# Odd layer of a two-layer encoder: S5 permutes through DRAM, S5 work cut into pieces, mask rows inside the score product

## The chip, the cores and the metric

The kernel runs on one core of one Trainium2 chip. It has five engines, each with its own instruction queue that is worked off in order: TensorE (PE, matrix products into PSUM, with its weight loads shown as PEld), VectorE (DVE), ScalarE (ACT), GpSimd (POOL) and SyncE (SP), which here does nothing but issue DMAs. ACT can issue DMAs too. The metric is the device time of one execution in microseconds (us), the median of several runs. Before the change it is 1480.8 us (three runs, 1479.17 to 1481.18).

## The reference, cut to what matters

Two residual layers over x of shape (512 positions, 1024 features). The even layer is Mamba-2 with differential attention, and a SwiGLU block follows each layer; none of that is edited. The odd layer projects once and feeds two groups:

```
u, c_q, c_kv, k_rope = split_cols(h @ w_in, (512, 384, 256, 32))
# S5: 32 groups of 16 channels, one 64-dim complex state per group
bu    = einsum('bsgh,gph->bsgp', ug, b_bar)
state = associative_scan(h_t = a_bar * h_{t-1} + bu_t)
y     = gelu(real(state @ c^T) + d_skip * ug);  y = y * sigmoid(y @ w_glu + b_glu)
# MLA: 8 heads, 64 plain + 32 rotary dims, block-causal mask in chunks of 64
q  = rms_norm(c_q) @ w_uq;  k_nope, v = split(rms_norm(c_kv) @ w_ukv)
p  = softmax(where(key_chunk <= query_chunk, (q . k) * scale, -inf));  o = p @ v
h  = h + concat(y, o) @ w_out
```

## The kernel before, in words

Activations are held feature-major: tiles of 128 features by 512 positions. Every projection is done in split precision (mm3, L173): weight and input are each cut into a high and a low part, and three products are summed per block of 128 input features, so a unit with 8 blocks is 24 matmuls (L178 to L180). The weights come as one DMA per chunk of one to four units (wload, L153) into one of two `raw` buffers; ACT makes the high part `whi` (L169), DVE the low part `wlo` (L170), each into one of two buffers, so the parts of a unit wait for the unit before last to be multiplied. `drive` (L244) walks a list of units and callbacks, and splits the weights of the next unit just before it writes the products of the present one. The list and a build-time scheduler fix the order of each engine's queue; at run time nothing is reordered.

The odd layer's list (L1475) is: four S5 input units `u`; `ck` twice, `cq` three times (the last of these and the key rotary part `cr` share a chunk); the row statistics of ck and cq (L309 sums of squares by a product with ones, a chain of some ten small DVE instructions, L326 a broadcast back); `values`; then the query and key units of the eight heads in four pairs; the GLU units; the attention steps, woven with the rest; the output units.

S5 is done in four quarters Q. `ev_u` (L1240) multiplies the projection by the row scale into `us`, and then sorts 16 blocks of 32 partitions by 128 columns into `u4` with 16 copies, half on ACT, half on DVE (L1247). `s5a` (L1252) makes eight products into two PSUM banks of the `sc` pair (L1258), four DVE products (L1266 to L1269), two POOL sums (L281), eight DVE scans (L1274), and the rotation back on DVE and POOL (L1284 to L1289). Two units later `s5b` (L1293) makes twelve products, adds the skip (L1305), applies GELU, and sorts blocks back into `yf`, again with 16 copies (L1311).

In an attention step (`scores`, L1392) each of two heads makes one score product with 96 rows (64 plain, 32 rotary; L1397), and a second product of one row that adds -1e30 to the last 64 columns of the first 64 queries (L1399); then a maximum on DVE, the exponential on ACT, and the division by the sum, on DVE for head 0 and on POOL for head 1 (L1405). `flip` transposes, `attend` multiplies by the values.

Of the kernel before, what the change touches and what calls it, by code (L numbers as in the profile page):

```python
# [121 lines left out]
class Trunk:  # L122
# [81 lines left out]

    def compute(self, u):
# [38 lines left out]
    def drive(self, items):  # L244
        us = [x for x in items if isinstance(x, dict)]
        nxt = {id(u): v for u, v in zip(us, us[1:])}
        self.prep(us[0])
        for x in items:
            if isinstance(x, dict):
                if id(x) in nxt:  # L250
                    self.prep(nxt[id(x)])
                self.compute(x)
            else:
                x()
        self.flush()
# [13 lines left out]
    def stat_add(self, st, src, pool=None, tag="sacc"):  # L269
        nc = self.nc  # L270
        if st["acc"] is None:
            st["acc"] = self.t(pool or self.stp, [P, T], tag)
            nc.scalar.activation(out=st["acc"], in_=src, func=AF.Square)
        else:
            sq = self.t(self.tmp, [P, T], "sq")
            nc.scalar.activation(out=sq, in_=src, func=AF.Square)
            self.padd(st["acc"], st["acc"], sq)

    def padd(self, out, x, y, op=ALU.add):
# [90 lines left out]
    def setup(self):  # L370
# [11 lines left out]
        self.n_unit = 0  # L382
        self.raws, self.kept = {}, {}
        self.queue, self.held = [], None
# [832 lines left out]
    def odd(self, E):  # L1217
# [7 lines left out]
        def start():  # L1225
            nonlocal sp
            sp = self.pool(ctx, "od")
            self.norm_done(E)

# [3 lines left out]
        def t5(tag, dt=F32):  # L1233

            return self.t(E["s5p"], [P, T], tag, dt)
# [4 lines left out]
        def ev_u(Q, ps):  # L1240
            us = t2("us", bufs=2)
            V.tensor_tensor(out=us.rearrange("p (i c) -> p i c", i=4), in0=ps.rearrange("p (c i) -> p i c", i=4),
                            in1=E["rbc"].rearrange("p (c i) -> p i c", i=4), op=ALU.mult)
            u4[Q] = t2(f"u4{Q}", shape=[P, 4, P])
            for q in range(4):
                for i in range(4):
                    (A.copy if i % 2 else V.tensor_copy)(out=u4[Q][32 * i:32 * i + 32, q, :],  # L1247
                                                         in_=us[32 * q:32 * q + 32, i * P:(i + 1) * P])

        def v4(x):  # L1250
            return x.rearrange("p (q c) -> p q c", q=4)[:, :, 0:P - 1]

        def s5a(Q):
            S = self.s5
            pb = [self.ps("sc") for _ in range(2)]
            for ri in range(2):
# [13 lines left out]
            self.padd(t[0], t[0], t[1])  # L1270
            self.padd(t[2], t[2], t[3], ALU.subtract)
            for q in range(4):
                for x in (t[0], t[2]):
                    V.tensor_tensor_scan(x[:, q * P:(q + 1) * P],  # L1274
                                         S["r4"][:, 4 * Q + q:4 * Q + q + 1].broadcast_to([P, P]),
                                         x[:, q * P:(q + 1) * P], 0.0, op0=ALU.mult, op1=ALU.add)
            c_, s_ = (S[n][Q].rearrange("p q c -> p (q c)") for n in ("rc", "rs"))
            if Q % 2:
                hr, hi = (t5(f"b{ri}{Q // 2}").rearrange("p (q c) -> p q c", q=4) for ri in range(2))
            else:  # L1280
                hr, hi = t2("hr", shape=[P, 4, P]), t2("hi", shape=[P, 4, P])
# [7 lines left out]
            G.tensor_tensor(out=hi[:, :, 1:P], in0=hi[:, :, 1:P], in1=v4(t[3]), op=ALU.add)  # L1289
            self.later(2, lambda: s5b(Q, hr, hi))  # L1290

        def s5b(Q, hr, hi):
            S = self.s5  # L1293
            ps = self.ps("sc")
# [13 lines left out]
            yf[Q] = t2(f"yf{Q}")  # L1308
            for j in range(4):
                for q in range(4):  # L1310
                    (A.copy if q % 2 else V.tensor_copy)(out=yf[Q][32 * q:32 * q + 32, j * P:(j + 1) * P],  # L1311
                                                         in_=yy[32 * j:32 * j + 32, q * P:(q + 1) * P])

# [61 lines left out]
        def ev_qk(m, n):  # L1375
            def f_(ps):
                if n == 0:
                    qk[m] = [None, None]
                x = qk[m][n] = [t5(f"{('b1', 'rc')[n]}{2 * (m % 2) + hh}") for hh in range(2)]
                for hh in range(2):  # L1380
# [10 lines left out]
        def scores(m, qb):  # L1391
# [15 lines left out]

# [67 lines left out]
        items = [start] + uu  # L1475
# [64 lines left out]
def pack(i):  # L1540
# [27 lines left out]
    def putc(n, v):  # L1568
# [11 lines left out]
    putc("sg64", np.where(r % 64 < 32, -tp, tp)[:, None])  # L1580
    putc("sg32", np.where(r % 32 < 16, -tp, tp)[:, None])
    putc("sel", (r[:, None] % 32 == np.arange(16)[None, :]) & (r[:, None] < 64))
# [3 lines left out]
    arrays = {"xt": i["x"][0].T, "positions": i["positions"], "par": par, "cst": cst, "mask": mask, "cidx": cidx,  # L1586
              "rowp": rowp, "s5bc": bc}
    mats = {n: i[n][0] for n in ("ev_w_in", "ev_w_out", "od_w_in", "od_w_glu", "od_w_uq", "od_w_ukv", "od_w_out")}
# [32 lines left out]
```

## Time and profile before

| | us |
|---|---|
| median of three runs | 1480.8 |
| profiled execution, its own time | 1481.41 |
| its span in the trace | 1479.6 |
| PE busy in the span | 1426.2 (96%) |
| DVE busy | 954.1 (64%) |
| ACT busy | 661.5 (45%) |
| POOL busy | 256.9 (17%) |

The page cuts the span into 40 slices of 37 us. A digit is the busy share of a slice in tenths, and PEclk the clock that TensorE was granted, in tenths of full speed. Only in the slices from about 880 to 990 us, the S5 and latent part of the odd layer, do both fall below 9 in the middle of the span. A matmul's busy time in the trace is longer than its share of the engine, since matmuls overlap; from one start to the next is the better measure.

### The profile page before, as it was taken

What the parts mean: (1) busy time and instruction counts of PE and PEld (TensorE: products, weight loads), DVE (VectorE), ACT (ScalarE), POOL (GpSimd) and SP (SyncE); (2) the same over time, 40 slices, a digit from 0 to 9 for tenths busy, and PEclk for the clock granted to TensorE, in tenths of its full rate; (3) what the DMA queues carried; (4) which work ended last, traced back from release to release, by engine and by line L of the source; (5) the groups of instructions that cost most, each with busy time, mean ns of one, the idle gap of its engine ahead of it and who ended that gap; (6) DMA issues with size and microseconds to landing.
All of it is one profiled execution on the core that took longest, in us unless ns stands there. A gap on an engine that the chain in (4) does not pass through costs nothing.

```text
span 1479.6 us, 18488 instructions
## 1 busy us (share of the span) xinstructions
PE 1426.2 (96%) x7043; PEld 1155.1 (78%) x7043; DVE 954.1 (64%) x1992; ACT 661.5 (45%) x1198; POOL 256.9 (17%) x206
## 2 busy tenths in 40 slices
PE   7999999999999999999999997789999999999997
PEld 5877877788878877888888886666688888888887
DVE  6987788777664999774634469886664433443453
ACT  5658766767544334334223453256453322222342
POOL 0234511000002210011011213523221100100111
PEclk9999999999999999999999998889999999999999
DMA  5221121112212222223222221020122232323221
GB/s 179 78 73 58 61 82 44 59 57 72 86 58 85 102 86 86 86 86 107 96 103 87 98 86 38 24 75 2 62 109 85 89 112 86 108 77 114 86 100 57
DMA packets 20248, 119.80 MB, mean 81 GB/s; under 512 B 2368, under 2 KB 3008, under 8 KB 9024
## 3 DMA queue, kind: packets, MB, share of 16 engines
q1 hardware_dynamic: 18864, 116.86, 22.9%
q10 hardware_dynamic: 1296, 1.76, 0.4%
q8 instruction: 55, 0.90, 0.3%
q14 instruction: 33, 0.27, 0.1%
HBM read 116.52 MB, written 2.10 MB: 80 GB/s over the span
## 4 chain that ended last, share of the span: by engine, by line
PE 74%; DVE 18%; ACT 3%; POOL 2%; issue 2%; DMA 1%; SPq 0%; ACTq 0%; DVEq 0%; POOLq 0%
PE mm L178 14%; PE mm L180 14%; PE mm L179 13%; PE sc L180 7%; PE sc L179 7%; PE sc L178 7%; DVE wlo L170 3%; PE sc L1397 1%; PE sc L813 1%; POOL xs L281 1%; PE po L842 1%; DVE qsw L608 1%; PE mm L750 1%; PE po L1425 1%; PE sc L812 1%
## 5 line engine op out<-in xcount | busy, mean ns | idle before, releaser
L169 ACT CAST whi<-raw 128x1024 fp32r<-128x1024 f32 (+5 forms) x231 | 223.9, 970 | 568.6 <-PE mm L179 331.3
L170 DVE TENSOR_TENSOR wlo<-raw,whi 128x1024 fp32r<-128x1024 f32 (+5 forms) x231 | 266.8, 1155 | 44.2 <-ACT whi L169 31.6
L281 POOL TENSOR_TENSOR gt<-gt,rbc 128x512 f32<-128x512 f32 x44 | 76.3, 1734 | 572.6 <-ACT gt L952 572.6
L957 DVE TENSOR_TENSOR gt<-mm,gt 128x512 f32<-128x512 f32 x44 | 30.3, 690 | 111.3 <-PE mm L180 107.9
L281 POOL TENSOR_TENSOR sacc<-sacc,sq 128x512 f32<-128x512 f32 x29 | 45.4, 1566 | 300.5 <-issue 232.7
L951 DVE TENSOR_TENSOR gt<-sc,rbc 128x512 f32<-128x512 f32 x44 | 30.3, 689 | 88.9 <-PE sc L180 88.9
L180 PE MATMUL mm<-x0h,wlo 128*128 128x512 f32 (+2 forms) x91 | 37.2, 409 | 12.4 <-DVE wlo L170 12.4
L178 PE MATMUL mm<-x0h,whi 128*128 128x512 f32 (+2 forms) x91 | 39.9, 438 | 6.1 <-ACT x0h L343 5.4
L972 DVE TENSOR_TENSOR h<-h,mm 128x512 f32<-128x512 f32 x20 | 13.7, 687 | 44.0 <-PE mm L180 44.0
L768 ACT ACTIVATE qsw<-mm 32x512 f32<-32x512 f32 x64 | 37.7, 589 | 3.1 <-DVE qraw L764 2.3
L972 DVE TENSOR_TENSOR h<-h,sc 128x512 f32<-128x512 f32 x20 | 13.7, 686 | 38.9 <-PE sc L180 38.8
L178 PE MATMUL mm<-x1h,whi 128*128 128x512 f32 (+2 forms) x91 | 36.7, 403 | 1.8 <-ACT x1h L343 1.8
L952 ACT ACTIVATE gt<-gt 128x512 f32<-128x512 f32 x44 | 27.6, 628 | 22.9 <-DVE gt L951 22.9
L180 PE MATMUL mm<-x1h,wlo 128*128 128x512 f32 (+2 forms) x91 | 37.3, 410 | 0.0
L180 PE MATMUL mm<-x2h,wlo 128*128 128x512 f32 (+2 forms) x91 | 37.2, 408 | 0.0
L178 PE MATMUL mm<-x7h,whi 128*128 128x512 f32 (+2 forms) x95 | 37.1, 391 | 0.0
L180 PE MATMUL mm<-x7h,wlo 128*128 128x512 f32 (+2 forms) x95 | 37.1, 391 | 0.0
L179 PE MATMUL mm<-x7l,whi 128*128 128x512 f32 (+2 forms) x95 | 37.0, 390 | 0.0
L179 PE MATMUL mm<-x0l,whi 128*128 128x512 f32 (+2 forms) x91 | 36.8, 405 | 0.2 <-DVE x0l L344 0.2
L179 PE MATMUL mm<-x2l,whi 128*128 128x512 f32 (+2 forms) x91 | 37.0, 407 | 0.0
L179 PE MATMUL mm<-x1l,whi 128*128 128x512 f32 (+2 forms) x91 | 36.8, 404 | 0.2 <-DVE x1l L344 0.2
L178 PE MATMUL mm<-x3h,whi 128*128 128x512 f32 (+2 forms) x91 | 36.8, 405 | 0.0
(938 smaller groups left out, 4385.5 us busy)
## 6 DMA issues: line engine op xcount, KB each, us to landing
raw<-in_f_dram SPq DMA_DIRECT2D x52, 1024.0 KB, 4.8
raw<-in_w_dram SPq DMA_DIRECT2D x35, 1024.0 KB, 4.8
raw<-in_f_dram SPq DMA_DIRECT2D x16, 896.0 KB, 4.5
raw<-in_w_dram SPq DMA_DIRECT2D x8, 512.0 KB, 3.6
h<-in_xt_dram SPq DMA_DIRECT2D x8, 256.0 KB, 6.8
raw<-in_w_dram SPq DMA_DIRECT2D x2, 640.0 KB, 3.9
out_dram<-otm SPq DMA_DIRECT2D x4, 256.0 KB, 2.5
out_dram<-otm ACTq DMA_DIRECT2D x4, 256.0 KB, 2.9
```

Source lines behind the costliest of these rows:

```text
L169: nc.scalar.copy(out=hi[:, :n], in_=raw[:, o:o + n])
L170: nc.vector.tensor_tensor(out=lo[:, :n], in0=raw[:, o:o + n], in1=hi[:, :n].bitcast(F32), op=ALU.subtract)
L178: nc.tensor.matmul(ps, lhsT=hi[:, k, :m], rhs=xh, start=start and j == 0, stop=False)
L179: nc.tensor.matmul(ps, lhsT=hi[:, k, :m], rhs=xl, start=False, stop=False)
L180: nc.tensor.matmul(ps, lhsT=lo[:, k, :m], rhs=xh, start=False, stop=stop and j == n - 1)
L281: self.nc.gpsimd.tensor_tensor(out=out, in0=x, in1=y, op=op)
L608: V.scalar_tensor_tensor(out=acc, in0=xr[:, 1 + k:1 + k + T], scalar=self.par("cw", 12 * k + j), in1=acc, op0=ALU.mult, op1=ALU.add)
L768: A.activation(out=sw[c * 32:(c + 1) * 32, :], in_=ps[d * 32:(d + 1) * 32, :], func=AF.Identity, scale=scale)
L951: V.tensor_tensor(out=gt, in0=ps, in1=E["rbc"], op=ALU.mult)
L952: A.activation(out=gt, in_=gt, func=AF.Silu)
L957: V.tensor_tensor(out=gt, in0=ps, in1=gt, op=ALU.mult)
L972: V.tensor_tensor(out=self.h[i], in0=self.h[i], in1=ps, op=ALU.add)
```

## The change

- `regroup` (new): the 16 copies of a block sort become one DMA of the tile (128 by 512, 256 KB) to a DRAM scratch tile and four DMAs back, each 32 partitions by 4 by 128 elements (64 KB). All five are issued by SP. It serves `u4` and `yf` of all four quarters: eight times, 40 DMAs.
- `s5a` becomes a generator in four pieces (products; scans; rotation back; second products with GELU), and the list places each piece. Its first products go to the PSUM pair `po`. Quarters 1 and 3 use other buffers for their result.
- `drive` counts the units left of each weight chunk and calls `fetch` before each unit, so that a chunk's DMA is written as soon as one of the two `raw` buffers has no unit left.
- The mask becomes four more rows of the score product (96 to 100), loaded by eight DMAs of 8 KB on ACT's queue into the query and key tiles of pairs 0 and 1; pairs 2 and 3 use the same tiles again. The one-row product goes.
- The division of head 1 goes from POOL to ACT.

The order of the engines' queues differs from before only between the odd layer's first units and its last attention steps (and in one mask load at the start).

```
+    def fetch(self):
+        for k in self.order:
+            if k not in self.raws:
+                if sum(self.left[x] > 0 for x in self.raws) >= 2:
+                    return
+                self.raws[k] = self.wload(k)
...
+    def regroup(self, out, src):
+        d = self.t(self.dram, [P, T], "regroup", bufs=4)
+        self.nc.sync.dma_start(out=d, in_=src)
+        for i in range(4):
+            self.nc.sync.dma_start(out=out[32 * i:32 * i + 32],
+                                   in_=d.rearrange("(q p) (i c) -> p i q c", q=4, i=4)[:, i])
...
             u4[Q] = t2(f"u4{Q}", shape=[P, 4, P])
-            for q in range(4):
-                for i in range(4):
-                    (A.copy if i % 2 else V.tensor_copy)(out=u4[Q][32 * i:32 * i + 32, q, :],
-                                                         in_=us[32 * q:32 * q + 32, i * P:(i + 1) * P])
+            self.regroup(u4[Q], us)
...
-            pb = [self.ps("sc") for _ in range(2)]
+            pb = [self.ps("po") for _ in range(2)]
...
             self.padd(t[2], t[2], t[3], ALU.subtract)
+            yield
             for q in range(4):
                 for x in (t[0], t[2]):
                     V.tensor_tensor_scan(x[:, q * P:(q + 1) * P],
...
-            self.later(2, lambda: s5b(Q, hr, hi))
-
-        def s5b(Q, hr, hi):
-            S = self.s5
+            yield
             ps = self.ps("sc")
...
+            self.regroup(yf[Q].rearrange("p (j c) -> p j c", j=4), yy)
...
+                if m < 2:
+                    x = [t5(f"{('b1', 'rc')[n]}{2 * (m % 2) + hh}") for hh in range(2)]
+                    for hh in range(2):
+                        A.dma_start(out=x[hh][96:100, :], in_=a["cmask"][4 * n:4 * n + 4, :])
+                else:
+                    x = qk[m - 2][n]
...
-                PE.matmul(ps[:, :n], lhsT=qk[m][0][hh][0:96, qb * P:(qb + 1) * P], rhs=qk[m][1][hh][0:96, :n],
-                          start=True, stop=False)
-                PE.matmul(ps[:, n - 64:n], lhsT=self.mrow, rhs=self.nrow, start=False, stop=True)
+                PE.matmul(ps[:, :n], lhsT=qk[m][0][hh][0:100, qb * P:(qb + 1) * P],
+                          rhs=qk[m][1][hh][0:100, :n], start=True, stop=True)
...
-            for hh, e in enumerate((V, G)):
-                e.tensor_scalar(out=pp[hh][:, :n], in0=pp[hh][:, :n], scalar1=rr[:, hh:hh + 1], scalar2=None,
-                                op0=ALU.mult)
+            V.tensor_scalar(out=pp[0][:, :n], in0=pp[0][:, :n], scalar1=rr[:, 0:1], scalar2=None, op0=ALU.mult)
+            A.mul(out=pp[1][:, :n], in_=pp[1][:, :n], mul=rr[:, 1:2])
...
-        items += [L(s5a, 0), uck[0], L(s5a, 1), uck[1], lambda: self.later(1, rows_k, rows_k2), ucq[0], L(s5a, 2),
-                  ucq[1], ucq[2], L(s5a, 3), lambda: self.later(1, rows_q, rows_q2)] + ukr
-        items += [uv, uqr(0)] + uqk(0) + uqk(1) + [uqr(1)]
+        items = [start] + uu[:3] + [s5(0), uu[3], s5(0), uck[0], s5(1, 0), uck[1], lambda: self.later(1, rows_k, rows_k2),
+                                    s5(1), ucq[0], s5(1), s5(0), ucq[1], s5(2), ucq[2], s5(2, 1),
+                                    lambda: self.later(1, rows_q, rows_q2)]
+        items += ukr + [s5(3, 2), uv, s5(3, 2), uqr(0), s5(3)] + uqk(0) + [s5(3)] + uqk(1) + [uqr(1)]
```

Three places in the queues. First SP, at the start of the odd layer; before, it holds weight chunks alone (`raw`):

```order
L157 DMA raw_7733<-in_w_dram 128x2048
L157 DMA raw_7857<-in_w_dram 128x2048
L157 DMA raw_8018<-in_w_dram 128x2048
L157 DMA raw_8226<-in_w_dram 128x1280
L157 DMA raw_8381<-in_w_dram 128x1408
```

Now, from the chunk of the first two cq units on, the block sorts of the four `u` quarters stand among the chunks, and then that of the first `yf`:

```order
L157 DMA raw_7797<-in_w_dram 128x2048
L298 DMA regroup_7778<-us_7775 128x512
L298 DMA regroup_7787<-us_7784 128x512
L300 DMA u_1443_7777<-regroup_7778 32x4x128 x4
L300 DMA u_1446_7786<-regroup_7787 32x4x128 x4
L298 DMA regroup_7827<-us_7824 128x512
L298 DMA regroup_7885<-us_7882 128x512
L157 DMA raw_7903<-in_w_dram 128x1280
L300 DMA u_1453_7826<-regroup_7827 32x4x128 x4
L300 DMA u_1465_7884<-regroup_7885 32x4x128 x4
L157 DMA raw_8014<-in_w_dram 128x1408
L298 DMA regroup_8102<-us_8095 128x512
```

SP works in order, so a `raw` that stands behind a sort waits for what the sort waits for, and a sort's reads wait for its write to land.

Second DVE, from the last `u` unit to the low part of the first ck unit (`us`: scaled projection; `t`: S5's working tiles; `rc`, `rs`: its rotation tables):

```order
L1247 COPY u_1455_7890<-us_7888 32x128 x8
L1266 TENSOR_TENSOR t_1458_7917<-sc_7907,rc_1132_5514 128x512
L1267 TENSOR_TENSOR t_1459_7918<-sc_7908,rs_1133_5515 128x512
L1268 TENSOR_TENSOR t_1460_7919<-sc_7908,rc_1132_5514 128x512
L1269 TENSOR_TENSOR t_1461_7920<-sc_7907,rs_1133_5515 128x512
L1274 SCALAR_TENSOR_TENSOR t_1458_7917<-s5r_1063_5005,t_1458_7917 128x128 x4
L1274 SCALAR_TENSOR_TENSOR t_1460_7919<-s5r_1063_5005,t_1460_7919 128x128 x4
L1284 TENSOR_TENSOR hr_7935<-t_1458_7917,rc_1132_5514 128x4x127
L1286 TENSOR_TENSOR hi_7936<-t_1460_7919,rc_1132_5514 128x4x127
L1288 TENSOR_TENSOR hr_7935<-hr_7935,t_1459_7918 128x4x127
L170 TENSOR_TENSOR wlo_7946<-raw_7857,whi_7945 128x1024
L344 SCALAR_TENSOR_TENSOR ck0l_7975<-mm_7949,par_94,ck0h_7974 128x512
```

Now (`po` in the place of `sc`):

```order
L1267 TENSOR_TENSOR us_7882<-mm_7857,rbc_7768 128x512
L170 TENSOR_TENSOR wlo_7900<-raw_7690,whi_7899 128x1024
L1289 TENSOR_TENSOR t_1457_7843<-po_7833,rc_1133_5516 128x512
L1292 TENSOR_TENSOR t_1460_7846<-po_7833,rs_1134_5517 128x512
L1290 TENSOR_TENSOR t_1458_7844<-po_7834,rs_1134_5517 128x512
L1291 TENSOR_TENSOR t_1459_7845<-po_7834,rc_1133_5516 128x512
L1298 SCALAR_TENSOR_TENSOR t_1457_7843<-s5r_1064_5007,t_1457_7843 128x128 x4
L1298 SCALAR_TENSOR_TENSOR t_1459_7845<-s5r_1064_5007,t_1459_7845 128x128 x4
L1310 TENSOR_TENSOR hr_7956<-t_1457_7843,rc_1133_5516 128x4x127
L1312 TENSOR_TENSOR hi_7957<-t_1459_7845,rc_1133_5516 128x4x127
L1314 TENSOR_TENSOR hr_7956<-hr_7956,t_1458_7844 128x4x127
L170 TENSOR_TENSOR wlo_7967<-raw_7797,whi_7966 128x1024
```

The copies are gone, the `wlo` of the second ck unit has moved ahead of quarter 0's products, and the `wlo` behind quarter 0 is that of the first cq unit.

Third PE, around the sum of squares of ck (`tp<-ones,sacc`); before, it stands behind the second products of quarter 1 (`sc<-u,tt`, `sc<-b,cx`) and ahead of those of quarter 2's first ones:

```order
L1298 MATMUL sc_8127<-b_1476_8008,cx_1144_5592 128x128
L1300 MATMUL sc_8127<-b_1477_8009,cx_1145_5593 128x128
L309 MATMUL tp_8163<-ones_97,sacc_7978 128x1 x4
L1258 MATMUL sc_8188<-u_1449_7840,b_1191_6065 128x128 x4
L178 MATMUL mm_8232<-x0h_7425,whi_8092 128x512
```

Now, behind the last products of the first cq unit and ahead of quarter 0's second products:

```order
L179 MATMUL mm_8016<-x7l_7673,whi_7966 128x512
L180 MATMUL mm_8016<-x7h_7672,wlo_7967 128x512
L333 MATMUL tp_8047<-ones_97,sacc_7934 128x1 x4
L1320 MATMUL sc_8082<-u_1443_7777,tt_1122_5429 128x128
L1321 MATMUL sc_8082<-hr_7956,cx_1095_5190 128x128
L1323 MATMUL sc_8082<-hi_7957,cx_1096_5191 128x128
```

The statistic has moved ahead of quarter 0's and quarter 1's second products and ahead of the second cq unit.

## Rows read from the trace of the kernel before

**Rows 1.** Windows: length, PE, PEld, DVE, ACT, POOL busy (count), PEclk, DMA share, GB/s.
```profile
882.00:988.00 106.00, 83.84 (x412) 67.66 (x411) 89.49 (x184) 41.33 (x88) 40.70 (x33) 0.87 0.11 36
988.00:1012.00 24.00, 23.22 (x111) 16.01 (x109) 20.04 (x33) 17.75 (x31) 6.83 (x5) 1.00 0.14 53
1012.00:1080.00 68.00, 68.00 (x399) 45.66 (x399) 41.44 (x94) 32.92 (x87) 16.22 (x14) 1.00 0.13 47
```
**Rows 2.** PE's waits from 882 to 1012 us: total, times, longest.
```profile
PE mm L180 <- DVE wlo L170: 12.1, 4, 6.1
PE tp L326 <- DVE rkr L319: 4.8, 1, 4.8
PE mm L178 <- DVE b L1382: 3.5, 1, 3.5
```
**Rows 3.** Timeline of PE: start, length, instruction.
```profile
882.02 1.95 PE L1258 MATMUL sc<-u,b 128*128 128x128 f32 x16
883.72 0.48 PE L178 MATMUL mm<-x0h,whi 128*128 128x512 f32 x1
...
889.26 1.95 PE L1258 MATMUL sc<-u,b 128*128 128x128 f32 x16
```
**Rows 4.** The chain that ended last: start, length, what; a matmul after a wait.
```profile
913.08 0.43 PE mm L178
```
**Rows 5.** Timeline of DVE, quarters 0 and 1 of S5.
```profile
885.25 0.69 DVE L1266 TENSOR_TENSOR t<-sc,rc 128x512 f32<-128x512 f32 x1
...
887.95 4.76 DVE L1274 TENSOR_TENSOR_SCAN t<-s5r,t 128x128 f32<-128x128 f32 x8 [0.21 <-POOL t L281]
...
895.47 2.27 DVE L170 TENSOR_TENSOR wlo<-raw,whi 128x1024 fp32r<-128x1024 f32 x1
897.66 0.74 DVE L344 SCALAR_TENSOR_TENSOR ck0l<-mm,par,ck0h 128x512 fp32r<-128x512 f32 x1
...
910.74 0.74 DVE L344 SCALAR_TENSOR_TENSOR ck1l<-mm,par,ck1h 128x512 fp32r<-128x512 f32 x1
```
**Rows 6.** Timeline of ACT.
```profile
911.51 0.60 ACT L276 ACTIVATE sq<-mm 128x512 f32<-128x512 f32 x1 [4.98 <-DVE ck1l L344]
912.12 1.28 ACT L1307 ACT_TABLE_LOAD   x1
913.42 0.63 ACT L1307 ACTIVATE us<-us 128x512 f32<-128x512 f32 x1
```
**Rows 7.** Timeline of POOL.
```profile
912.18 1.27 POOL L281 TENSOR_TENSOR sacc<-sacc,sq 128x512 f32<-128x512 f32 x1 [2.37 <-ACT sq L276]
...
960.05 2.51 POOL L1330 TENSOR_TENSOR cx<-us,rope_cos 32x512 f32<-32x512 f32 x1
962.64 3.02 POOL L1332 TENSOR_TENSOR cx<-cx,hi 32x512 f32<-32x512 f32 x1
```
**Rows 8.** Windows of lines L1247 and L1311, the copies: length, DVE, ACT busy.
```profile
870.00:988.00 118.00, 6.96 (x32) 9.50 (x32) 0.88 0.12 41
882.00:988.00 106.00, 7.94 (x32) 9.48 (x32) 0.87 0.11 36
```
**Rows 9.** DMA issues: count, KB each, median us from issue to landing.
```profile
raw<-in_w_dram SPq DMA_DIRECT2D x35, 1024.0 KB, 4.8
...
out_dram<-otm SPq DMA_DIRECT2D x4, 256.0 KB, 2.5
...
cidx<-in_cidx_dram SPq DMA_DIRECT2D x1, 64.0 KB, 3.0
```
**Rows 10.** Timeline of SP at the start: four issues in a row.
```profile
1.16 1.84 SPq L409 DMA_DIRECT2D h<-in_xt_dram  x4
```
**Rows 11.** Line L1399, the mask product: count, ns; and two rows of PE's timeline.
```profile
L1399 PE MATMUL sc<-nrow,mrow x32: 197/198/199, 999.0 to 1071.4; 1*128 1x64 bf16 x32
...
1017.00 0.20 PE L1399 MATMUL sc<-nrow,mrow 1*128 1x64 bf16 x1
1017.13 0.44 PE L1415 MATMUL tp<-cst,rs 128*128 128x128 f32 x2
```

More of the change, by code (lines that the diff above doesn't have):

```diff
@@ L200, in prep @@
         o = sum(CH[u["key"]][2][:u["sub"]])
+        self.left[u["key"]] -= 1
         u["w"] = self.wsplit(self.raws[u["key"]], o, u["nk"], u["m"], u["keep"])
@@ L246, in drive @@
         nxt = {id(u): v for u, v in zip(us, us[1:])}
+        seen = set()
+        for u in us:
+            if u["keep"] is None or u["keep"] not in seen:
+                self.left[u["key"]] = self.left.get(u["key"], 0) + 1
+            seen.add(u["keep"])
+        self.order = list(self.left)
         self.prep(us[0])
@@ L251, in drive @@
                     self.prep(nxt[id(x)])
+                self.fetch()
                 self.compute(x)
@@ L382, in setup @@
         self.n_unit = 0
-        self.raws, self.kept = {}, {}
+        self.raws, self.kept, self.left = {}, {}, {}
         self.queue, self.held = [], None
@@ L1227, in start @@
             sp = self.pool(ctx, "od")
+            self.dram = self.pool(ctx, "swap", space=bass.MemoryType.DRAM)
             self.norm_done(E)
@@ L1276, in s5a @@
                                          x[:, q * P:(q + 1) * P], 0.0, op0=ALU.mult, op1=ALU.add)
-            c_, s_ = (S[n][Q].rearrange("p q c -> p (q c)") for n in ("rc", "rs"))
-            if Q % 2:
-                hr, hi = (t5(f"b{ri}{Q // 2}").rearrange("p (q c) -> p q c", q=4) for ri in range(2))
+            yield
+            if Q == 1:
+                hr, hi = (t5(f"b{ri}0").rearrange("p (q c) -> p q c", q=4) for ri in range(2))
+            elif Q == 3:
+                hr, hi = (t2(f"t{ri}", shape=[P, 4, P]) for ri in range(2))
             else:
@@ L1289, in s5a @@
             G.tensor_tensor(out=hi[:, :, 1:P], in0=hi[:, :, 1:P], in1=v4(t[3]), op=ALU.add)
-            self.later(2, lambda: s5b(Q, hr, hi))
-        def s5b(Q, hr, hi):
-            S = self.s5
+            yield
             ps = self.ps("sc")
@@ L1308, in s5b @@
             yf[Q] = t2(f"yf{Q}")
[L1309 to L1312, printed above, removed]
+            self.regroup(yf[Q].rearrange("p (j c) -> p j c", j=4), yy)
         cq, ck = [None] * 3, [None] * 2
@@ L1378, in f_ @@
                     qk[m] = [None, None]
-                x = qk[m][n] = [t5(f"{('b1', 'rc')[n]}{2 * (m % 2) + hh}") for hh in range(2)]
+                if m < 2:
[4 more added lines that the diff above has]
+                    x = qk[m - 2][n]
+                qk[m][n] = x
                 for hh in range(2):
@@ L1474, in odd, with s5, f_ @@
         uv = self.unit("vq", 0, None, None, body=values)
-        items = [start] + uu
-        items += [L(s5a, 0), uck[0], L(s5a, 1), uck[1], lambda: self.later(1, rows_k, rows_k2), ucq[0], L(s5a, 2),
-                  ucq[1], ucq[2], L(s5a, 3), lambda: self.later(1, rows_q, rows_q2)] + ukr
-        items += [uv, uqr(0)] + uqk(0) + uqk(1) + [uqr(1)]
+        gens = {}
+        def s5(*Qs):
+            def f_():
+                for Q in Qs:
+                    if Q not in gens:
+                        gens[Q] = s5a(Q)
+                    next(gens[Q], None)
+            return f_
+        items = [start] + uu[:3] + [s5(0), uu[3], s5(0), uck[0], s5(1, 0), uck[1], lambda: self.later(1, rows_k, rows_k2),
+                                    s5(1), ucq[0], s5(1), s5(0), ucq[1], s5(2), ucq[2], s5(2, 1),
+                                    lambda: self.later(1, rows_q, rows_q2)]
+        items += ukr + [s5(3, 2), uv, s5(3, 2), uqr(0), s5(3)] + uqk(0) + [s5(3)] + uqk(1) + [uqr(1)]
         steps = [(m, qb) for m in range(4) for qb in (3, 2, 1, 0)]
@@ L1581, in pack @@
     putc("sg32", np.where(r % 32 < 16, -tp, tp)[:, None])
+    cm = np.zeros((8, T), f)
+    for b in range(4):
+        cm[b, P * b:P * b + 64] = 1.0
+        cm[4 + b, P * b + 64:P * b + P] = NEG
     putc("sel", (r[:, None] % 32 == np.arange(16)[None, :]) & (r[:, None] < 64))
@@ L1586, in pack @@
     arrays = {"xt": i["x"][0].T, "positions": i["positions"], "par": par, "cst": cst, "mask": mask, "cidx": cidx,
-              "rowp": rowp, "s5bc": bc}
+              "rowp": rowp, "s5bc": bc, "cmask": cm}
     mats = {n: i[n][0] for n in ("ev_w_in", "ev_w_out", "od_w_in", "od_w_glu", "od_w_uq", "od_w_ukv", "od_w_out")}
```

## The prediction

> **What bounds the kernel now.** I read the page's slices first: PE is busy 9 tenths or more nearly everywhere, and in the stretch that the change reorders (the S5 and latent part of the odd layer) it is not. The windows put numbers to it [rows 1]: from 882 to 988 us PE is busy 83.84 of 106 us, so 22.2 us are idle, and the granted clock is 0.87; from 988 (the GLU units) to 1080 PE is busy without a gap worth the name, at clock 1.00. The waits say what PE lacked [rows 2]: four times the low part of a weight, 12.1 us, the longest 6.1; once `rkr`, the end of the ck statistic, 4.8; once an attention operand, 3.5. That is 20.4 of the 22.2 us.
>
> A matmul after a wait starts every 0.43 us [rows 4]; between waits a unit of 24 takes 889.26 - 883.72 = 5.54 us, 0.23 each [rows 3]. These fit the two clock levels, 1.2 and 2.4 GHz. A mean of 0.87 between 0.5 and 1.0 means up to 13.8 us lost to the low level (0.13 x 106); some of it falls in idle time, so I take 12.5, or 2.1 for each of the six waits. What remains of the stretch is PE's work at full clock: 106 - 22.2 - 12.5 = 71.3 us.
>
> Why `wlo` is late shows in DVE's timeline [rows 5]. From 885.25 DVE works off a quarter of S5 (products, scans 4.76, rotation); the `wlo` that PE wants stands behind it at 895.47. A quarter's chain up to `ck0l` lasts 897.66 + 0.74 - 885.25 = 13.15 us, two of them up to `ck1l` 26.2 us. DVE is 84% busy (89.49 of 106), so the stretch is a contest between DVE's chain and the order in which PE asks for things.
>
> **The change, part by part.** The profiled execution took 1481.41 us (median 1480.8); the sum is made against it.
>
> *Sorts.* The copies go: in 882 to 988 us 7.94 us of DVE and 9.48 of ACT for `yf`, 6.96 and 9.50 for `u4` [rows 8]. The `u4` copies lay beside the products of the `u` units, so PE gains nothing from them directly. In their place stand five DMAs per sort. No such round trip is in the trace; by the nearest rows a 256 KB store lands in 2.5 us, a 64 KB load in 3.0 [rows 9], and SP needs 0.46 per issue [rows 10]: 2.5 + 4 x 0.46 + 3.0 = 7.3 us. From below: 64 KB pieces of data that is already at hand could take no longer than the store, so 5; from above, where it stands behind a 1 MB chunk (4.8, rows 9) 7.3 + 4.8 = 12.1. I take 7.3, nearest to rows of the same size, plus the chunk for the first sort. The first `u4` sort has its chunk ahead of it and the reads land at about 883 to 884, when PE has the last `u` unit behind it and wants them: hidden to within a microsecond. The others have a unit or more (5.54 each) as cover; without it each would cost its 7.3.
>
> *Pieces.* I laid PE's new order from 882.0, with the same 71.3 us of work. DVE's chain starts about 885.0, since `wlo` of the second ck unit (2.27, rows 5) now stands ahead of it; so the 6.1 us wait disappears, and other things are late next:
> 1. The first cq unit wants a bank that `ck0l` and ACT's square empty: 885.0 + 13.15 + 0.6 (the products are taken in another order) + 0.60 [rows 6] = 899.4. PE gets there at 882.0 + 2 x 5.54 + two of `s5a`'s product sets at 1.7 (883.72 - 882.02, rows 3) = 896.5. Hole 2.9.
> 2. The ck statistic now stands right behind that unit and ahead of quarter 0's second products, so a wait is added with the rest of PE's queue behind it. It needs `ck1l` (885.0 + 26.2 = 911.2), the square 0.60 and POOL's sum 1.27 [rows 7]: 913.1. PE is there at 899.4 + 5.54 + 2.1 (low level after the hole) = 907, or 905 if less of it is low. Hole 6 to 8, taken as 6.8, with hole 1's loss of clock hidden in it.
> 3. The cq statistic, behind the last cq and the key unit: 0.7.
> 4. `yf` of an early quarter comes by DMA, and ACT's cast of it stands ahead of the emptying of a bank: 1.2.
> 5. The cq row waits for `rqr`, which stands on DVE behind quarter 3's scans, and these behind POOL's rotation of the key, 2.51 + 3.02 [rows 7]; the mask DMAs on ACT's queue wait at the same time for tiles that S5 frees. Hole 3.1; its bounds are 0 (POOL early) and 5.5 (all of POOL's two steps).
> Holes 2.9 + 6.8 + 0.7 + 1.2 + 3.1 = 14.7; low level after holes 2 and 5, 2 x 2.1 = 4.2. The GLU units start at 882.0 + 71.3 + 14.7 + 4.2 = 972.2 instead of 988: gain 15.8.
>
> *GLU and first attention.* From 988 to 1012 us ACT was busy 17.75 of 24, PE 23.22 [rows 1]. ACT now also has six of the 16 divisions of head 1 (at most 0.60 each, the square of the same tile size, rows 6: 3.6) and, since exponential, sigmoid and GELU alternate there, three more table loads of 1.28 [rows 6], 3.8. 17.75 + 7.4 = 25.2 is more than the stretch: ACT becomes the bound in it. Loss between 0 (the casts are elsewhere by then) and 4.5 (every load in front of PE); I take 2.5. In the trace the next activation follows 0.02 us after the load's end [rows 6]. The Trainium skill speaks against this part: "ScalarE: Activation LUTs", section "What ACT_TABLE_LOAD costs", gives about 2.66 us for each switch, load and drain together. By it the three switches would cost about 4 us more (3 x 1.38), and the estimate would be 1469; this trace shows no such drain, so the sum stays with 1.28.
>
> *Mask.* 32 one-row products go. Each shows 198 ns, but from its start to the next product's it is 0.13 us [rows 11]. Six of them fall before 1012, the other 26 into a stretch in which PE is all that counts (68.00 of 68, rows 1): 26 x 0.13 = 3.4 us. The longer contraction (100 rows for 96) streams as many columns, and I cost it at nothing. The eight 8 KB DMAs take ACT 8 x 0.46 = 3.7 us at SP's rate, beside PE's work (counted in 5 where they are not). The divisions after 1012 find ACT at 32.92 of 68.
>
> *Early weight DMAs* cost nothing while two chunks are in hand; no wait of [rows 2] is for a chunk, so nothing is gained.
>
> Sum: -15.8 + 2.5 - 3.4 = -16.7, 1464.7 against the profiled execution, 1464 to 1465 by the median. I say 1465; this likeliest case by itself spans 1456 to 1473: downwards hole 2 at 2 and hole 5 at nothing (4.8 + 3.1), upwards both at their upper ends (1.2 + 2.4), the GLU loss at 4.5 (2.0) and one sort uncovered by its chunk (4.8 at most, of which I count half).
>
> **The rivals.** *DVE's chain decides.* It begins no earlier (885.0 for 885.25), and if DVE has little slack through four quarters, PE only waits elsewhere; what is left is the mask, 4 us, and a little more: 1475 to 1478. For it: DVE is busy 89.49 of 106, and hole 2 is the old chain under another name. Against it: 7.94 us of copies leave DVE in just this stretch.
>
> *ACT or the round trip holds.* ACT's queue stops at a cast of `yf` that has not landed or at a mask DMA, twice for 3 to 4 us, with 2.1 of low clock after each: 10 us of the gain go, 1475. For it: SP's order puts chunks behind sorts, ACT now mixes DMAs with casts. Against it: ACT is idle for 61% of the stretch.
>
> *Nearly everything is won.* All idle time, all low clock and the masks would give 1481.4 - 22.2 - 12.5 - 4.1 = 1442.6; if hole 2 shrinks to 2 and 5 vanishes, 1455 or lower, about 1452. For it: removed DVE work is 15 us with the `u4` copies. Against it: `ck1l` at about 911 rests on DVE's durations.
>
> *Slower: the sorts come in series on PE's path.* Eight sorts at 7.3 us, each with 2.1 of low clock where it stops PE. The sum gives 16.7 us away to spend: from the second sort that is not hidden at all (2 x 9.4 = 18.8) the change loses. Two: 1483.5; three: 1493. For it: SP works in order, reads wait for the write's landing, a late sort delays the chunk behind it and with it the next unit. Against it: a sort's consumer is a unit or more away, and two chunks are in hand.
>
> *The change does not do what it says:* the one-row products gone but the holes unmoved is the first rival; I give it no chance of its own.
>
> **How the numbers follow.** Likeliest case 0.58; DVE's chain 0.12; ACT or round trip 0.13; nearly everything 0.09; slower 0.08. What a measurement of this kernel can tell from no change is about 0.2%, 3 us. Faster by more than that: all cases but the slower one, 0.92, less 0.05 of the DVE case that ends at 1478 or just above and so within the 0.2%, and less 0.01 of the ACT case, should its stops be twice as long; 0.86. No change 0.05, slower 0.08 + 0.01 = 0.09. The range leaves out the slower case and the far end of the good one: 1452 to 1478.
>
> **What would show it.** Right: no wait ahead of the second ck unit; a wait of about 3 us ahead of the first cq unit, for DVE's `ck0l` or ACT's square; one of 6 to 8 us at the ck statistic, ended by POOL's sum; about 3 at the cq row; sorts of 2.5 and 3.0 us; GLU at about 972; six table loads; attention as full of PE as before. Wrong: waits that end with a sort's DMA, or with a weight chunk (rival four); ACT stopped at a mask DMA for more than 4 us with PE behind it; a GLU start before 965 or after 980; or a ck statistic that finds `ck1l` done, which would mean that DVE's chain starts or runs earlier than I read.

## The result and the profile after

The changed kernel takes 1461.45 us (four runs, 1458.52 to 1462.28) against 1480.03 before: ratio 0.987, 95% interval 0.9853 to 0.9888, so 18.6 us less. The prediction was 1465, with a range of 1452 to 1478. The profiled execution spans 1460.5 us, 19.1 less than that of before.

The windows of the trace after, cut at the events of [rows 1] (the first is the S5 part and ends where the GLU units start, the second ends where the score products of the second pair of heads begin, the third where the last attention product starts):

```profile
880.60:972.40 91.80, 79.18 (x412) 65.96 (x411) 75.99 (x141) 28.46 (x46) 39.73 (x33) 0.91 0.23 75
972.40:1002.00 29.60, 25.38 (x118) 18.38 (x116) 20.68 (x40) 24.47 (x43) 2.95 (x2) 0.88 0.17 58
1002.00:1060.80 58.80, 58.80 (x357) 43.49 (x355) 39.85 (x90) 37.18 (x96) 0.00 (x0) 1.00 0.15 55
```

Before, cut at the same events (the first of the three windows is in [rows 1]):

```profile
988.00:1014.70 26.70, 25.92 (x132) 17.93 (x130) 21.90 (x37) 19.97 (x38) 7.52 (x5) 1.00 0.13 47
1014.70:1079.60 64.90, 64.90 (x375) 43.54 (x373) 39.33 (x89) 30.30 (x81) 15.53 (x13) 1.00 0.14 50
```

The cuts stand at the same events, but the work between them is not quite the same: the last six products of a key unit (two blocks of L178 to L180, 0.23 us each, 1.4 in all) lie ahead of the second cut before, and behind it now. Their first one, before and after:

```profile
1002.44 0.39 PE L178 MATMUL mm<-ck0h,whi 128*128 128x512 f32 x1
1004.75 0.50 PE L178 MATMUL mm<-ck0h,whi 128*128 128x512 f32 x1
```

The reader is to see three things. The S5 part is 14.2 us shorter (106.0 to 91.8), with the same 412 matmuls, less DVE (89.49 to 75.99) and less ACT. The GLU part is 2.9 longer, 4.3 for the same work; its clock is 0.88 where it was 1.00, and ACT fills 24.47 of 29.60. The attention part is 6.1 shorter, 7.5 for the same work, although PE is full in both. 14.2 - 2.9 + 6.1 = 17.4; the rest is 0.3 in the tail and 1.4 to 1.5 at the very start, where the profiled execution of before waited longer for its second input tile. The first projection with 128 outputs starts at 13.66 us in the trace of before, at 12.11 in that of the change, and at 12.03 to 12.04 with the mask rows alone and the sorts alone, whose start is ordered as before: so this belongs to the execution and not to the change. The long stretch from there to the odd layer's first units, which no edit touches, differs between the traced executions as well, by up to 1.9 us. So lengths between two events are compared below, and not times from the start of a trace.

PE's waits in the same part after (total, times, longest):

```profile
PE tp L333 <- POOL sacc L305: 7.1, 1, 7.1
PE mm L178 <- ACT sacc L289: 2.2, 1, 2.2
PE sc L1423 <- ACT rs L1426: 2.2, 2, 1.6
PE tp L350 <- DVE rqr L343: 1.9, 1, 1.9
PE sc L1323 <- POOL hi L1315: 1.0, 1, 1.0
PE mm L178 <- ACT us L1466: 1.0, 1, 1.0
PE tp L1439 <- ACT tt L1440: 0.7, 1, 0.7
```

No wait for a `wlo` is left [rows 2]. What is late now is the ck statistic (first line), the bank that the first cq unit wants (second), and the cq row (fourth): the three that the prediction named. The other four lines are a POOL rotation and, in the GLU part, three waits for ACT.

The chain behind the first of them, in DVE's, ACT's and POOL's timelines (start, length, instruction), against [rows 5 to 7]:

```profile
881.79 1.22 DVE L170 TENSOR_TENSOR wlo<-raw,whi 128x1024 fp32r<-128x1024 f32 x1
882.93 0.69 DVE L1289 TENSOR_TENSOR t<-po,rc 128x512 f32<-128x512 f32 x1
...
896.00 0.74 DVE L368 SCALAR_TENSOR_TENSOR ck0l<-mm,par,ck0h 128x512 fp32r<-128x512 f32 x1
...
907.43 0.74 DVE L368 SCALAR_TENSOR_TENSOR ck1l<-mm,par,ck1h 128x512 fp32r<-128x512 f32 x1
```

```profile
908.20 0.60 ACT L292 ACTIVATE sq<-mm 128x512 f32<-128x512 f32 x1 [9.24 <-DVE ck1l L368]
```

```profile
908.87 1.42 POOL L305 TENSOR_TENSOR sacc<-sacc,sq 128x512 f32<-128x512 f32 x1 [0.25 <-ACT sq L292]
```

The chain is the predicted one, with the same steps, only from 882.93 where 885.0 was read: 2.3 us behind the start of the part (880.60) and not 3.0, since the `wlo` ahead of it took 1.22 us where 2.27 was read. PE had ended the first cq unit at 903 and stood until the sum was there:

```profile
897.49 0.50 PE L178 MATMUL mm<-x0h,whi 128*128 128x512 f32 x1 [2.25 <-ACT sacc L289]
897.82 0.39 PE L179 MATMUL mm<-x0l,whi 128*128 128x512 f32 x1
898.05 0.40 PE L180 MATMUL mm<-x0h,wlo 128*128 128x512 f32 x1
...
910.34 1.87 PE L333 MATMUL tp<-ones,sacc 128*128 128x1 f32 x8 [7.12 <-POOL sacc L305]
...
951.78 2.07 PE L350 MATMUL tp<-cst,rqr 128*128 128x128 f32 x8 [1.85 <-DVE rqr L343]
953.65 0.63 PE L1320 MATMUL sc<-u,tt 128*128 128x128 f32 x2
954.08 0.64 PE L1321 MATMUL sc<-hr,cx 128*128 128x128 f32 x2
```

After 2.25 us of waiting the matmuls start 0.23 apart, at the high level; after the 7.12, and after the 1.85 that follow closely on another wait of 1.0, each of the instructions shown as x2 is 0.43 behind the one ahead of it, where the same ones of quarter 1, at 930.62 to 933.07, are 0.22 apart: so the low level.

### The profile page after: what moved, and what is told of

Its sections match the earlier page's. It is cut to its first block, busy times and chain, and to the rows that moved or that the text cites. A ratio compares the mean times of both kernels' runs of the same rounds, so it can differ in the third digit from the quotient of the medians.

```text
span 1460.5 us, 18355 instructions
## 1 busy us (share of the span) xinstructions
PE 1413.4 (97%) x7011; PEld 1152.3 (79%) x7011; DVE 936.0 (64%) x1928; ACT 653.0 (45%) x1153; POOL 236.0 (16%) x190
## 4 chain that ended last, share of the span: by engine, by line
PE 74%; DVE 17%; ACT 4%; issue 2%; POOL 2%; DMA 1%; SPq 0%; DVEq 0%; ACTq 0%; POOLq 0%
PE mm L178 14%; PE mm L179 13%; PE mm L180 13%; PE sc L180 7%; PE sc L179 7%; PE sc L178 7%; DVE wlo L170 3%; DVE qsw L632 2%; PE sc L837 1%; PE sc L1423 1%; POOL xs L305 1%; PE po L866 1%; PE po L1449 1%; PE mm L774 1%; PE sc L836 1%
## 5 line engine op out<-in xcount | busy, mean ns | idle before, releaser
L178 PE MATMUL mm<-x0h,whi 128*128 128x512 f32 (+2 forms) x91 | 39.6, 435 | 9.4 <-ACT x0h L367 5.5
L180 PE MATMUL mm<-x0h,wlo 128*128 128x512 f32 (+2 forms) x91 | 36.4, 400 | 3.6 <-DVE wlo L170 3.6
L178 PE MATMUL mm<-x7h,whi 128*128 128x512 f32 (+2 forms) x95 | 37.1, 390 | 0.0
L180 PE MATMUL mm<-x7h,wlo 128*128 128x512 f32 (+2 forms) x95 | 37.0, 390 | 0.0
L180 PE MATMUL mm<-x1h,wlo 128*128 128x512 f32 (+2 forms) x91 | 36.5, 401 | 0.0
L179 PE MATMUL mm<-x1l,whi 128*128 128x512 f32 (+2 forms) x91 | 36.3, 399 | 0.2 <-DVE x1l L368 0.2
L178 PE MATMUL mm<-x1h,whi 128*128 128x512 f32 (+2 forms) x91 | 36.0, 396 | 0.2 <-ACT x1h L367 0.2
L180 PE MATMUL mm<-x2h,wlo 128*128 128x512 f32 (+2 forms) x91 | 36.2, 397 | 0.0
L179 PE MATMUL mm<-x3l,whi 128*128 128x512 f32 (+2 forms) x91 | 35.9, 394 | 0.3 <-DVE x3l L365 0.3
```

The source lines that it names most:

```text
L178: nc.tensor.matmul(ps, lhsT=hi[:, k, :m], rhs=xh, start=start and j == 0, stop=False)
L179: nc.tensor.matmul(ps, lhsT=hi[:, k, :m], rhs=xl, start=False, stop=False)
L180: nc.tensor.matmul(ps, lhsT=lo[:, k, :m], rhs=xh, start=False, stop=stop and j == n - 1)
```

## The experiments

The kernel before stood at 1479.25 to 1479.49 us beside these runs, and the ratios are against that. Two medians that lie less than 3 us apart are, by the prediction's own measure, not told apart; for those the traces have to speak.

### Parts taken back from the changed kernel

**u4 sorts by copies again** (`self.regroup(u4[Q], us)` becomes the 16 copies).

> The changed kernel (1461.45 us) with the four u4 sorts done by 16 copies each again, eight on DVE and eight on ACT; the yf sorts stay with the DMAs. Theory (the u4 copies lay beside products, and only those of the last u unit reach DVE's chain): the chain of quarter 0 starts 8 x 0.22 = 1.7 us later than its 882.93, the two waits behind it (2.25 and 7.12 us) grow by as much together, and the time is 1462 to 1464. Rival 1 (the DVE time taken away is what the change won): 7 us of DVE come back, 1467 to 1469. Rival 2 (the round trips cost PE or SP something): 1460 or less.

Measured: 1461.58 (0.9876, 0.9859 to 0.9894). Nothing moved: the copies lay beside products, as the theory has it, and even the 1.7 us are not seen (the theory's range began at 1462).

**yf sorts by copies again.**

> The changed kernel with the four yf sorts done by copies again, the u4 sorts by DMA. Theory: 2 us of DVE and 2.4 of ACT per quarter come back; quarters 0 and 1 lie in DVE's chain ahead of the rows of cq and the rotations, so the waits at the cq row (1.85 us) and behind it grow, with one stretch of low clock: 1463 to 1467. Rival 1 (each sort that DVE does again is a wait of its own with 2 us of low clock): 1473 or more. Rival 2 (the casts that wait for a yf to land cost more than the copies): 1460 or less.

Measured: 1469.42 (0.9929, 0.9915 to 0.9943), 8 us more, above the theory's 2 to 6 and below the first rival. Its waits of PE beside those of the changed kernel:

```profile
PE sc L1320 <- ACT b L1387: 3.6, 1, 3.6
PE mm L180 <- DVE wlo L170: 2.5, 1, 2.5
...
PE mm L178 <- ACT whi L169: 2.0, 1, 2.0
```

All three are new or grown: ACT and DVE, busy with copies, are late with the values and the weights. The S5 part (881.46 to 981.24 here) lasts 99.8 us against 91.8, so the whole loss lies in it. The yf sorts are the half of that edit that counts.

**One-row mask products again** (their rows still loaded).

```
-  matmul(ps[:, :n], lhsT=q[0:100, ...], rhs=k[0:100, :n], start=True, stop=True)
+  matmul(ps[:, :n], lhsT=q[0:96, ...], rhs=k[0:96, :n], start=True, stop=False)
+  matmul(ps[:, n - 64:n], lhsT=self.mrow, rhs=self.nrow, start=False, stop=True)
```

> The changed kernel with 96 rows in each score product and the 32 one-row mask products back; the mask rows are still loaded. Theory of the prediction (a one-row product costs its 0.13 us from start to start): 32 x 0.13 = 4.1, 1465 to 1466. Rival (it also keeps the next score product from starting under the one before: two score products of 512 columns take 0.91 us apiece in the trace of the changed kernel against 1.06 + 0.13 before): 32 x 0.2 or more, 1468 to 1470. If the rows were worth nothing: 1461.

Measured: 1474.67 (0.9963, 0.9946 to 0.9981), 13 us more. Its ten runs spread from 1468.3 to 1478.2, and with them goes the granted clock, from 0.992 to 0.982; at 0.988 they take 1471.4 to 1473.1, where the changed kernel takes 1461.3 to 1462.3 at 0.987 to 0.989: 10 us more at the same clock. The predicted 0.13 us a product is refuted. The attention part of the trace (1002.00 to 1060.80 in the changed kernel), with otherwise the same products in it, lasts 66.90 with 24 of the mask products, 8.1 more, or 0.34 each; the GLU part ahead lasts 3.6 more, at a clock of 0.85:

```profile
971.20:1004.40 33.20, 29.68 (x126) 19.26 (x125) 21.71 (x41) 25.45 (x45) 2.95 (x2) 0.85 0.15 51
1004.40:1071.30 66.90, 66.90 (x380) 44.76 (x379) 39.78 (x88) 37.29 (x94) 0.00 (x0) 1.00 0.14 48
```

**The same with a float32 mask product** (`mrow` and `nrow` in the type of the scores).

> The changed kernel with 96 rows in each score product and a one-row mask product in float32, the type of the score product, where it was bfloat16 (1474.67 us, span 1471.2). Theory 1 (the change of type between two products is what keeps the next one back): the products stand in a row like the 100-row ones and cost little more than 0.13 us each: 1464 to 1467. Theory 2 (any further product in the group costs its slot and a drain, whatever its type): 1470 to 1476, with the same 1.06 us for 512 columns as before. The float32 product of 64 columns may itself be longer, about 0.2 us in place of 0.13: 2 us more.

Measured: 1481.41 (1.0018, 0.9991 to 1.0045). The twelve runs fall in two groups, six of 1474 to 1477 at a granted clock of 0.990 to 0.993 and six of 1486 to 1493 at 0.978 to 0.983. The first theory falls by either; the first group lies close to the 1470 to 1476 of the second. The two score products of a step over 512 keys, in the kernel before, in the changed one, and here (PE's timeline; a matmul of float32 shows as two instructions):

```profile
1014.75 1.13 PE L1397 MATMUL sc<-rc,b 96*128 96x512 f32 x2
1015.81 0.20 PE L1399 MATMUL sc<-nrow,mrow 1*128 1x64 bf16 x1
1015.94 1.12 PE L1397 MATMUL sc<-rc,b 96*128 96x512 f32 x2
```

```profile
1002.03 1.98 PE L1423 MATMUL sc<-rc,b 100*128 100x512 f32 x4
1003.85 0.38 PE L1439 MATMUL tp<-cst,rs 128*128 128x128 f32 x2
```

```profile
1000.86 1.12 PE L1428 MATMUL sc<-rc,b 96*128 96x512 f32 x2
1001.91 0.43 PE L1430 MATMUL sc<-nr,mr 1*128 1x64 f32 x2
1002.27 1.13 PE L1428 MATMUL sc<-rc,b 96*128 96x512 f32 x2
```

Before, both heads take 2.38 us (1014.75 to 1017.13, [rows 11]); now 1.82; so 0.28 per mask product at this length, of which its own row shows 0.13. The other 0.15 hide in the score product, 1.06 with a mask product behind it and 0.91 in a row with its like. With float32 the score product takes the same 1.05, and the mask product 0.36. So it is the product in between that lengthens the score product, whatever its type; the type shows in the mask product's own row. The number of rows, 96 or 100, which also differs, does not do it: the one score product of before that stands without its mask product (985.02) and its counterpart of the changed kernel (969.45) are both 1.09 us ahead of the start of the second product behind them:

```profile
985.02 1.02 PE L1397 MATMUL sc<-rc,b 96*128 96x512 f32 x2
986.11 0.40 PE L179 MATMUL mm<-cq0l,whi 128*128 128x512 f32 x1
...
969.45 1.02 PE L1423 MATMUL sc<-rc,b 100*128 100x512 f32 x2
970.54 0.40 PE L179 MATMUL mm<-cq0l,whi 128*128 128x512 f32 x1
```

**Division of head 1 on POOL again.**

> The changed kernel with the division of head 1 back on POOL. Theory (ACT bounds the stretch of the GLU units and first attention steps, with four table loads between 980 and 994 us): six divisions of 0.5 to 0.7 us leave ACT there, 1459 to 1460. Rival 1 (POOL's division is slower and its result comes later to the transposes): 1462 to 1464. Rival 2: ACT waits on its table loads alone, and nothing moves: 1461.

Measured: 1459.42 (0.9866, 0.9849 to 0.9884), 2 us less, as the theory has it, but below the 3 us that medians can tell. The trace bears it out: the GLU part ends at 997.2 after 26.1 us, with its clock at 1.00, against 29.6 at 0.88.

```profile
971.10:997.20 26.10, 23.13 (x116) 16.13 (x115) 19.87 (x37) 22.25 (x37) 7.08 (x5) 1.00 0.20 68
```

Some of it goes again in the attention part, which lasts 60.3 us (to 1057.46) after 58.8; in it stand some transposes that lay in the GLU part before, and a wait of PE for POOL of 0.7. Together the two parts are 2.1 us shorter.

**No early issue of weight DMAs** (`self.fetch()` taken out).

> The changed kernel without the early issue of weight DMAs; a chunk is issued where its first unit is split, as before, and the mask load at the start stands where it stood before. Theory (no wait of PE was for a chunk): 1460 to 1463; and if the 1.4 us at the start of the trace come from the place of the mask load, 1463. Rival (behind the sorts on SP a chunk is late without it): 1466 or more.

Measured: 1462.53 (0.9882, 0.9866 to 0.9899; 1457.3 to 1463.0). No difference that can be told. The mask load at the start stood where it stood before, and the first wide projection still started earlier than in the trace of before (12.75 against 13.66).

### Parts put alone into the kernel before

**Mask rows alone.**

> The kernel before with the mask rows alone: four more rows in the score products, their eight loads on ACT's queue, no one-row products; everything else as before, the division of head 1 on POOL. Prediction's price (0.13 us a product): 1476. Price read from the run with the products put back into the changed kernel (8.1 us for the last 24, 0.34 each): 32 x 0.34 = 10.9, 1469. If ACT's eight loads stop it there with PE behind: 1472 or more.

Measured: 1472.70 (0.9954, 0.9941 to 0.9967), 6.8 us less, with an attention part of 58.30 where it was 64.90. Four products of the key unit (0.9 us) stand in it that stood ahead of it before, so for the same work it is 7.5 us shorter by 24 mask products, 0.31 each.

```profile
1011.10:1069.40 58.30, 58.30 (x357) 42.86 (x355) 39.45 (x91) 29.96 (x84) 14.35 (x13) 1.00 0.16 55
```

So three readings of the attention part agree, 0.31 here and in the changed kernel (7.5 for 24) and 0.34 where the products were put back, and 32 of them are 10 to 11 us: the 10 that putting them back cost at the same clock. That this run wins only 6.8 is the GLU part's doing: it lasts 26.2 us (984.88 to 1011.10) where it lasted 26.8, although eight mask products and four of the key unit have left it, and ACT has five table loads of 1.28 in it instead of two, which is the likely reason. So the further table loads come with the mask rows alone too. Why the runs with the products put back were granted a lower clock in some executions stays open.

**Sorts alone.**

> The kernel before with its eight sorts by DMA and nothing else. Theory (DVE's chain ahead of wlo loses 2 us of copies per quarter, in the order of before too): 1471 to 1476. Rival 1 (in the order of before the copies lie beside PE's waits or behind the chain): 1478 to 1480. Rival 2 (the round trip is late, since a u4 is wanted right behind its unit there): 1482 or more.

Measured: 1469.64 (0.9937, 0.9924 to 0.9949), 9.8 us less, more than the theory had; the S5 part (880.49 to 975.99) lasts 95.5 us. The wait for `wlo` shrinks from 12.1 [rows 2] to 1.7, while one of 6.0 in the values unit, for ACT's `b`, comes up:

```profile
PE sc L1363 <- ACT b L1367: 6.0, 1, 6.0
PE tp L334 <- DVE rkr L327: 4.5, 1, 4.5
...
PE mm L180 <- DVE wlo L170: 1.7, 2, 1.4
```

**Pieces alone** (changed kernel with copies, mask products, POOL's division).

> The changed kernel with all sorts by copies, the one-row mask products and the division of head 1 on POOL: of the change only the pieces, their places and the early weight DMAs are left. If the parts add up (yf sorts 8 us, mask rows 10 to 13, ACT's division -2, u4 sorts nothing): 1461.45 + 8 + 10 to 13 - 2 = 1477 to 1481, as before. Rival 1 (the new order fills holes by itself): 1468 to 1473. Rival 2 (the new order needs the DMAs, and with the copies DVE is late everywhere): 1483 or more.

Measured: 1474.57 (0.9971, 0.9960 to 0.9983), 4.9 us less; between the theory and the first rival. Its S5 part lasts 99.3 us (879.45 to 978.73), 6.7 less than before; the two parts behind it lose 2.1 of that, with six table loads on ACT in place of two in the GLU part.

The parts nearly add up: -4.9 (pieces) - 9.8 (sorts) - 6.8 (mask rows) + 2.0 (ACT's division) = -19.5, measured -18.6. In the S5 part they do not: sorts alone make it 10.5 us shorter and pieces alone 6.7, both together 14.2, so they win part of the same time.

### A later statistic

**The ck statistic one unit later.**

```
-  lambda: self.later(1, rows_k, rows_k2),
+  lambda: self.queue.extend([[2, rows_k], [3, rows_k2]]),
```

> The changed kernel (1461.45 us) with the ck statistic one unit later: behind the second cq unit, ahead of quarter 2's first products; its row one unit behind it. Theory (PE waits 7.12 us for POOL's sum, and the 14 products behind it run at the low level): PE goes on to quarter 0's second products and then waits for the bank that ck1 leaves (908.8 us) instead of 910.34 and the slow products; the second cq unit starts near 909 in place of 917. Some of the 8 us comes back at the cq row, whose chain hangs on DVE: 1454 to 1458. Rival (DVE's chain decides, the wait only moves to the next unit or the cq row): 1460 to 1462.

Measured: 1456.03 (0.9845, 0.9832 to 0.9857), 5.4 us under the changed kernel, as the theory says. In its trace, where the S5 part begins at 879.05, the 7.1 us are gone; the second cq unit starts at 907.30, 28.3 us into the part, where it started 36.3 into it (916.91):

```profile
907.30 0.50 PE L178 MATMUL mm<-x0h,whi 128*128 128x512 f32 x1 [2.96 <-ACT sq L292]
```

and the S5 part takes 87.6 us at a clock of 0.96, 4.2 less than in the changed kernel; the GLU part (to 995.07) takes 28.4, 1.2 less:

```profile
879.05:966.64 87.59, 76.86 (x411) 63.00 (x410) 76.31 (x141) 28.41 (x46) 39.85 (x33) 0.96 0.24 78
```

**With the division on POOL too.**

> The changed kernel with the statistic one unit later and the division of head 1 on POOL again. If the two are independent, the 2 us of the division (1459.42 against 1461.45) come on top of what the later statistic gives: 1452 to 1456. If both only move PE ahead of the same ACT work in the GLU stretch, no more than the later statistic alone.

Measured: 1455.38 (0.9836, 0.9823 to 0.9849), 0.7 us under the later statistic alone, which is less than medians can tell. By the traces the GLU and attention parts together are 0.9 us shorter than with the later statistic alone (86.35 and 87.22), where POOL's division had brought 2.1: so it does not come on top in full.

**With two banks for ck and the row later still.**

> The changed kernel with the ck statistic one unit later and its row two units later, the ck units in alternating PSUM banks (so that the first cq unit finds a free one), and the division of head 1 on POOL. Theory (after the statistic is out of the way DVE's chain decides: the wait ahead of the first cq unit, 2.2 us, goes, and the one ahead of the second grows by as much): 1453 to 1456, as with the later statistic alone (1456.0) or 1 to 2 below. Rival (the waits are PE's own and add up): 1449 to 1452.

Measured: 1454.00 (0.9835, 0.9821 to 0.9848), the lowest of all, though not by more than medians can tell from the two before it. As the theory has it, the wait ahead of the first cq unit is gone, and the one ahead of the second has grown to 4.7 and that at the cq row to 3.5:

```profile
PE mm L178 <- ACT sq L292: 4.7, 1, 4.7
PE tp L350 <- DVE rqr L343: 3.5, 1, 3.5
```

The S5 part takes 86.7 us, 0.9 less than with the later statistic alone: most of the 2.2 us that went ahead of the first unit came back ahead of the second and at the cq row. Both waits end with DVE's work (ACT's `sq` here starts when `ck1l` is done, at 906.86), so with the statistic moved DVE's chain is the bound of this part.

## Why the prediction was right, step by step

*S5 part.* GLU units at 972.2 were predicted, and they stand at 972.37; that they agree so closely is luck, since three sizes in it were off and made up for each other. The stretch began 1.4 us earlier. The waits came to 12.5 us (7.1 + 2.2 + 1.9 + 1.0 + 0.3) instead of 14.7. Of 91.8 us, 71.3 of work and 12.5 of waits leave 8.0 for the low level, where 4.2 was counted; the clock says the same (0.09 x 91.8 = 8.3). The part itself became 14.2 us shorter and not 15.8. The mechanism, a contest between DVE's chain and PE's order in which the waits for `wlo` turn into other ones, is shown by the waits: 2.25 us ahead of the first cq unit where 2.9 was predicted, 7.12 at the ck statistic where it was 6.8, and 1.85 at the cq row, with 1.0 just ahead of it, where it was 3.1. That hole 2 was the new order's own price is shown by the later statistic.

*Sorts.* The `u4` copies were read as covered, and are (1461.58). For `yf` the prediction counted the copies as DVE's and ACT's time and gave them no price of their own; with copies in their place again the kernel takes 8 us more.

*GLU part.* 2.5 us of loss were predicted; the window shows 2.9, but for the same work it is 4.3, and that although eight mask products have left the part. So the term was too small, and the near hit again owes something to luck. ACT is the bound there, as POOL's division shows. The load at 980.12 starts 0.02 us after the end of the cast ahead of it (979.48, 0.62 long) and lasts 1.28, and the next activation follows at 981.41:

```profile
980.12 1.28 ACT L1466 ACT_TABLE_LOAD   x1
981.41 1.27 ACT L1466 ACTIVATE us<-mm,par 128x512 f32<-128x512 f32 x2
```

So the drain that the Trainium skill gives for a switch ("ScalarE: Activation LUTs", section "What ACT_TABLE_LOAD costs"), by which the estimate would have been 1469, is not seen here. There are six loads from 882 us on, as counted.

*Mask.* This is the term that was mis-sized most: 3.4 us predicted for 26 products, 7.5 measured for 24. The 0.13 us from the one-row product's start to the next is only what stands in its own row; 0.15 more, at 512 keys, lay in the length of the score product beside it. The prediction said that the longer contraction costs nothing, which holds, but took the score product's 1.06 as given.

*The sum.* Predicted: -15.8 + 2.5 - 3.4 = -16.7. Measured between the two traces: -14.2 + 4.3 - 7.5 = -17.4, and 1.7 more from the start of the trace and its tail, which the change does not explain. So each term had its mechanism right and its size off, by 1.6, 1.8 and 4.1 us, and the errors cancel in part.

*Round trips.* Stores landed in 2.1 us, reads in 2.0 (`u4`) and 3.1 (`yf`), against 2.5 and 3.0:

```profile
regroup<-us SPq DMA_DIRECT2D x8, 256.0 KB, 2.1
...
u<-regroup SPq DMA_DIRECT2D x16, 64.0 KB, 2.0
yf<-regroup SPq DMA_DIRECT2D x16, 64.0 KB, 3.1
```

No wait of PE ends with one, so the slower rival did not come near. One cast of `yf` on ACT waited 1.1 us for its read (at 944.99), and PE 0.3 behind it, where 1.2 was predicted. The mask loads stopped ACT for 5.8 us:

```profile
948.90 0.50 ACT L169 CAST whi<-raw 128x384 fp32r<-128x384 f32 x1
955.19 0.26 ACTq L1402 DMA_DIRECT2D rc<-in_cmask_dram  x1
```

That is more than the 4 us that the prediction set as a sign against it, but PE was not behind it: its two waits in that time, 1.0 and 1.85 us, ended with POOL and with DVE.

*The rivals.* DVE's chain alone: not here, but it decides once the statistic is moved. Nearly everything won: it wanted hole 2 down at 2 us; with the later statistic a wait of 3.0 stands in its place, at 1456, and the last version reaches 1454.

## What to carry to other kernels

A small product between two others is to be priced from the group, start of the first to start of what follows the last, with and without it, and not from its own row. An edit whose predicted terms sum up well may hold errors that cancel; windows cut at the same events tell, once it is checked that the same products lie between the cuts. A statistic whose chain runs over three engines is worth trying one unit further back than the first place where its inputs are due: that gave 5.4 us here, a fifth of the 25.5 us that the last version gained over the kernel before.

## What the runs showed of the hardware

A one-row product after each score product lengthened that product from 0.91 to 1.06 us at 512 keys, in bfloat16 and float32 alike; over all lengths of keys the bfloat16 product cost 0.31 to 0.34 us, where its own row shows 0.13.

A wait of 2.25 us left the clock at its high level, one of 7.12, and one of 1.85 that followed closely on another of 1.0, were followed by the low one. Waits of 2.69 us in the kernel before and of 2.96 with the later statistic lie between: matmuls went on 0.23 apart for some 1.5 us and were then 0.43 apart.

A load of ACT's tables took 1.28 us, and the next activation started 0.01 us behind it. Ten executions of one kernel ran from 1468.3 us at a granted clock of 0.992 to 1478.2 at 0.982.
